# Alpha of the RWKV recurrence loaded by parity into the tile of its product, and r loaded in rows of 1 KB

## Chip, cores and metric

The kernel runs on one core of one Trainium2 chip. The core has TensorE (PE in the profile, with its weight loads as PEld), VectorE (DVE), ScalarE (ACT), GpSimd (POOL) and SyncE (SP), which only issues DMAs here. The metric is the device time of one launch in microseconds, as the median of three runs.

## What is computed

Two layers of an encoder trunk run over 768 tokens (a sequence of 512 and one of 256) with 1024 features. Layer 0 has differential attention (4 heads) and, beside it, a bidirectional RWKV-7 mixer (8 heads of 64), with one output projection for both; layer 1 has dilated attention; each layer ends with a SwiGLU FFN. The change lies in the recurrence of the mixer, which runs forwards and backwards and is summed:

```python
def rwkv_scan(r, w, k, v, kk, a, reverse):
    def step(st, inp):
        r_t, w_t, k_t, v_t, kk_t, a_t = inp
        sa = jnp.einsum('bhvk,bhk->bhv', st, -kk_t)
        st = (st * w_t[:, :, None, :] + sa[..., None] * (kk_t * a_t)[:, :, None, :]
              + v_t[..., None] * k_t[:, :, None, :])
        y = jnp.einsum('bhvk,bhk->bhv', st, r_t)
        return st, y
    _, ys = lax.scan(step, s0, xs, reverse=reverse)
...
y = (rwkv_scan(rh, heads(decay(w0_f, w1_f, w2_f)), heads(k_f), vh, kk, heads(a_f), False)
     + rwkv_scan(rh, heads(decay(w0_b, w1_b, w2_b)), heads(k_b), vh, kk, heads(a_b), True))
```

## The kernel before

The recurrence runs in chunks of 64 tokens: 12 chunks in each direction, 24 units. An earlier stage has worked out, for each chunk, four operands with the decay folded in, and parked them in DRAM: alpha (`AL`, kk with the decay), r (`RH`), the two keys (`KB`, which holds kk·a and k side by side), and `Ti`, the inverse of a triangular matrix. Eight heads lie as four pairs `j` on the free axis; the parity `par` of a head says whether it lies on partitions 0 to 63 or 64 to 127 (`rows`).

A unit has three parts. `fetch` (L938 to L953) issues its DMAs on SP's queue: KB, two halves of RH, AL, two halves of v into the tile `SUV`; `fetch_inverse` (L955) adds Ti. RH goes into one of four standing tiles `rdiag` (L934), 128 x 4 x 128, that hold r on the diagonal blocks and zeros beside them, zeroed once by POOL, so that one matmul over 128 rows serves both heads of a pair. `prep` (L958 to L985) makes what does not depend on the state: the product of KB and RH on PE (bank `pp`, later `gm`), masked by DVE into `LR` (L969); a copy of alpha into `LK` by ACT, one for each parity (L973), and the product of KB and AL, masked by DVE into the other half of LK (L980); KB turned by PE and copied by ACT into `KBT` (L985). `chain` (L987 to L1028) is the serial part: the state S is copied into SUV (L996, one half by ACT and one by DVE), LK and SUV are multiplied into X, ACT copies X to `Xs` (L1001), Ti and Xs give U, copied into SUV (L1008, ACT and DVE), KBT and SUV give the new state (L1014 and the decay in L1015, both DVE), and RH with S plus LR with SUV give y, which goes into `ys` (L1024 by DVE, L1026 by ACT). When both directions have passed a block of 128 tokens, `finish` (L1029 on) normalizes it: a dozen instructions, most on DVE (L1037 to L1050), two on POOL.

`rounds` (L1064) walks the 24 units, forwards and backwards in turn, fetches three units ahead and prepares two ahead. The order on each engine is made by a scheduler that simulates the program with its own estimates when it is built: `chain` has a high priority, `prep` a low one, and the f32r matmuls of projections the lowest, as filling. The first five rounds share the time with the differential attention of the last heads; the other seven run while the weights of the output projection are loaded (`wo`, through `raw` at L134, two buffers) and split into a high and a low part (`split`: ACT's cast at L139, then a subtraction at L140, which for these eight weights is on POOL).

Of the kernel before, what the change touches and what calls it, by code (L numbers as in the profile page):

```python
# [8 lines left out]
F32 = mybir.dt.float32  # L9
F32R = mybir.dt.float32r  # L10
BF16 = mybir.dt.bfloat16
I32 = mybir.dt.int32
# [6 lines left out]
P = 128  # L19
# [35 lines left out]
class Core:  # L55
# [860 lines left out]
    def rwkv(self, rw, park, out):  # L916

        nc, A = self.nc, self.A
        am = []
        for d in "fb":  # L920
            t = rw.tile([P, P], I32, tag="am" + d, name="am" + d)
# [5 lines left out]
        tile = lambda tag, shape, bufs=1: rw.tile(shape, F32, tag=tag, name=self.uid(tag), bufs=bufs)  # L927
# [5 lines left out]

        rdiag = [rw.tile([P, 4, P], F32, tag=f"RH{i}", name=f"RH{i}") for i in range(NB)]  # L934
        for x in rdiag:
            nc.gpsimd.memset(x, 0.0)

        def fetch(di, c):  # L938
            u = {}
            u["AL"] = tile("AL", [P, 4, 64], NB)  # L940
            u["KB"] = tile("KB", [P, 4, 2, 64], NB - 1)
            u["SUV"] = tile("SUV", [P, 4, 2, 64], NB)
            n = units[0]
            units[0] += 1
            u["RH"], u["Ti"] = rdiag[n % NB], tile("Ti", [P, 4, 64], NB)
            nc.sync.dma_start(u["KB"], park["KB"][di, c])
            for rr in rows:
                nc.sync.dma_start(u["RH"][rr, :, rr], park["RH"][di, c, rr])
            nc.sync.dma_start(u["AL"], park["AL"][di, c])
            v = park["v"][64 * c:64 * c + 64].rearrange("t (j h v) -> t j h v", j=4, h=2)  # L950
            nc.sync.dma_start(u["SUV"][64:P, :, 0], v[:, :, 0])
            nc.sync.dma_start(u["SUV"][0:64, :, 1], v[:, :, 1])
            ready[di, c] = u  # L953
# [4 lines left out]
        def prep(di, c):  # L958

            u = ready[di, c]  # L960
            LK, LR, KBT = (tile(n, [P, 4, 2, 64], NB - 1) for n in ("LK", "LR", "KBT"))
            u["LK"], u["LR"], u["KBT"] = LK, LR, KBT
            KB, RH, AL = (u[n] for n in ("KB", "RH", "AL"))
            st = lambda x, j: x[:, j].rearrange("p s t -> p (s t)")
            b = self.bank("pp")
            for j in range(4):
                self.mm(b[:, j * P:(j + 1) * P], st(KB, j), RH[:, j])
            v = b.bitcast(I32).rearrange("p (j x) -> p j x", x=64)
            nc.vector.tensor_tensor(out=LR.rearrange("p j h x -> p (j h) x").bitcast(I32), in0=v,  # L969
                                    in1=am[di][:, 64:P].unsqueeze(1).to_broadcast([P, 8, 64]), op=ALU.bitwise_and)  # L970
            for par in range(2):
                rr = rows[par]
                nc.scalar.copy(out=LK[rr, :, par], in_=AL[rr])  # L973
            b = self.bank("pp")
            for j, par in heads:
                self.mm(b[rows[1 - par], j * 64:(j + 1) * 64], KB[rows[par], j, 1 - par], AL[rows[par], j])
            v = b[:, 0:256].bitcast(I32).rearrange("p (j x) -> p j x", x=64)
            for par in range(2):
                rr = rows[par]
                nc.vector.tensor_tensor(out=LK[rr, :, 1 - par].bitcast(I32), in0=v[rr],  # L980
                                        in1=am[di][rr, 0:64].unsqueeze(1).to_broadcast([64, 4, 64]), op=ALU.bitwise_and)
# [5 lines left out]
        def chain(di, c, first, last):  # L987
# [10 lines left out]
            for j, par in heads:  # L998
                self.mm(xb[rows[par], j * 64:j * 64 + 64], LK[:, j, par], SUV[:, j, par])
            X = tile("Xs", [P, 256], 2)  # L1000
# [18 lines left out]
            for j, par in heads:  # L1019
                y = yb[o, j * P + par * 64:j * P + par * 64 + 64]  # L1020
                self.mm(y, RH[:, j, rows[par]], S[:, j], True, False)
                self.mm(y, LR[:, j, par], SUV[:, j, par], False, True)
# [611 lines left out]
```

## Time and profile before

| what | value |
|---|---|
| runs | 2123.34, 2125.56, 2126.11 us, median 2125.56 |
| the profiled execution | 2126.21 us, its span 2124.4 us |
| PE busy | 2048.7 us, 96% of the span |
| DVE busy | 1378.2 us, 65% |
| ACT busy | 905.9 us, 43% |
| POOL busy | 886.5 us, 42% |
| mean granted TensorE clock | 0.973 of full speed |
| DMA packets | 150227, of them 95926 under 512 B |

The profile is of one execution. A time such as 621.67 counts from the start of its span. Busy time is an average over stages that are bound by different engines, so it says little by itself: what matters is who ends PE's waits in the stretch where the change lies. In a row of waits the engine on the left of the arrow waited, and what stands on the right came last. A row with several shapes gives a mean over them.

### The profile page before, as it was taken

How to read it: one execution, taken by the hardware profiler on the slowest of the kernel's cores; microseconds unless marked ns; L12 is line 12 of the kernel's file. 1: busy time of each engine (PE TensorE's matmuls, PEld its weight loads, DVE VectorE, ACT ScalarE, POOL GpSimd, SP SyncE). 2: the span in 40 equal slices, each digit the busy share in tenths (PEclk: the TensorE clock that was granted, in tenths of full speed). 3: DMA queues.
4: the chain of work that ended last, by engine and by line, in shares of the span. 5: the costliest groups of instructions: out<-in, count | busy, mean ns of one | idle time of the engine just before them, and what ended most of it. 6: DMA issues, size and time to landing. Idle time of an engine off the chain costs nothing. (4 is left out here: it accounts for less than half of the span.)

```text
span 2124.4 us, 33739 instructions
## 1 busy us (share of the span) xinstructions
PE 2048.7 (96%) x13270; PEld 1772.5 (83%) x13270; DVE 1378.2 (65%) x2147; ACT 905.9 (43%) x1703; POOL 886.5 (42%) x833
## 2 busy tenths in 40 slices
PE   7999999999998989999999999999998999999998
PEld 7767776777887778999999998888677999999997
DVE  5456996856579566566666657543568566666665
ACT  5467555447554254433333335222444433333332
POOL 4344341653113156543444535443137544543442
PEclk9999997999999999999999999999999999999999
DMA  4334434114365311211222235221131222221124
GB/s 156 87 75 90 97 74 137 55 26 144 84 184 161 129 64 61 80 60 60 73 77 70 72 137 193 74 71 38 51 109 60 71 79 70 70 69 60 60 80 149
DMA packets 150227, 189.01 MB, mean 89 GB/s; under 512 B 95926, under 2 KB 107784, under 8 KB 150068
## 3 DMA queue, kind: packets, MB, share of 16 engines
q1 hardware_dynamic: 126880, 168.00, 25.4%
q10 hardware_dynamic: 20372, 12.03, 2.0%
q0 software_dynamic: 2816, 6.83, 1.0%
q8 instruction: 104, 1.70, 0.3%
q14 instruction: 55, 0.45, 0.1%
HBM read 150.20 MB, written 36.23 MB: 88 GB/s over the span
## 5 line engine op out<-in xcount | busy, mean ns | idle before, releaser
L83 PE MATMUL gm<-xh,w 128*128 128x384 f32 x896 | 249.1, 342 | 2.8 <-ACT xh L139 2.8
L140 DVE TENSOR_TENSOR wl<-wraw,wh 128x1024 fp32r<-128x1024 f32 (+1 forms) x96 | 126.0, 1313 | 151.7 <-ACT wh L139 150.3
L83 PE MATMUL gm<-T,w 128*128 128x384 f32 x1032 | 203.6, 340 | 7.9 <-ACT w L139 7.3
L83 PE MATMUL gm<-xh,wh 128*128 128x256 f32 (+3 forms) x640 | 208.8, 348 | 0.8 <-ACT pad L489 0.8
L83 PE MATMUL gm<-xl,wh 128*128 128x256 f32 (+3 forms) x640 | 207.6, 348 | 0.0
L83 PE MATMUL gm<-xh,wl 128*128 128x256 f32 (+3 forms) x640 | 206.1, 346 | 0.0
L140 DVE TENSOR_TENSOR w<-S,w 128x512 fp32r<-128x512 f32 x176 | 168.8, 961 | 43.8 <-ACT w L139 36.4
L83 PEld LDWEIGHTS gm<-T,w 128*128 128x128 f32 x1032 | 184.1, 188 | 12.7 <-ACT w L139 8.5
L139 ACT CAST wh<-wraw 128x1024 fp32r<-128x1024 f32 (+1 forms) x103 | 107.5, 1046 | 163.8 <-PE gm L83 96.8
L139 ACT CAST w<-S 128x512 fp32r<-128x512 f32 x176 | 108.9, 621 | 156.7 <-POOL S L291 54.6
L83 PEld LDWEIGHTS gm<-xh,w 128*128 128x128 f32 x896 | 167.3, 192 | 7.7 <-ACT xh L139 3.6
L139 ACT CAST w<-wraw 128x512 fp32r<-128x512 f32 x126 | 76.0, 620 | 206.7 <-PE gm L83 138.1
L83 PE MATMUL gm<-xl,w 128*128 128x384 f32 x448 | 153.4, 342 | 3.0 <-DVE xl L140 3.0
L293 POOL TENSOR_TENSOR S<-wraw,S 128x512 f32<-128x512 f32 x42 | 62.8, 1496 | 204.8 <-DVE w L140 204.8
L140 DVE TENSOR_TENSOR w<-wraw,w 128x512 fp32r<-128x512 f32 x126 | 117.5, 949 | 38.1 <-ACT w L139 37.9
L83 PE MATMUL sc<-xh,w 128*128 128x384 f32 x512 | 140.8, 336 | 1.0 <-DVE u L330 1.0
L83 PEld LDWEIGHTS gm<-xh,wh 128*128 128x128 f32 (+1 forms) x640 | 120.2, 194 | 21.8 <-issue 5.8
L83 PEld LDWEIGHTS gm<-xh,wl 128*128 128x128 f32 (+1 forms) x640 | 119.9, 194 | 20.6 <-issue 7.0
L83 PEld LDWEIGHTS gm<-xl,wh 128*128 128x128 f32 (+1 forms) x640 | 120.0, 194 | 19.7 <-issue 7.3
L392 DVE TENSOR_TENSOR acc<-acc,ob 128x512 f32<-128x512 f32 x128 | 87.4, 683 | 66.6 <-PE ob L83 65.5
L83 PE MATMUL sc<-T,w 128*128 128x384 f32 x552 | 111.2, 340 | 7.4 <-ACT v L350 3.3
L348 POOL TENSOR_TENSOR sil<-sil,v 128x384 f32<-128x384 f32 x44 | 46.9, 1066 | 163.1 <-DVE v L330 162.9
(502 smaller groups left out, 5301.5 us busy)
## 6 DMA issues: line engine op xcount, KB each, us to landing
wraw<-in_gate SPq DMA_DIRECT2D x44, 512.0 KB, 3.4
wraw<-in_down SPq DMA_DIRECT2D x44, 512.0 KB, 3.7
wraw<-in_up SPq DMA_DIRECT2D x40, 512.0 KB, 3.5
wraw<-in_wqk SPq DMA_DIRECT2D x20, 512.0 KB, 3.7
wraw<-in_wo SPq DMA_DIRECT2D x14, 512.0 KB, 4.0
wraw<-in_wrkv SPq DMA_DIRECT2D x12, 512.0 KB, 3.5
KB<-pkKB SPq DMA_DIRECT2D x24, 256.0 KB, 3.2
pkx<-x SPq DMA_DIRECT2D x12, 512.0 KB, 3.4
```

The source lines that it names most:

```text
L83: return self.nc.tensor.matmul(o, a, b, start=start, stop=stop)
L139: self.nc.scalar.copy(out=hi, in_=x)
L140: (eng or self.nc.vector).tensor_tensor(out=lo, in0=x, in1=hi.bitcast(F32), op=ALU.subtract)
L293: eng.tensor_tensor(out=s2, in0=a12, in1=s2, op=ALU.subtract)
L348: nc.gpsimd.tensor_tensor(out=o, in0=o, in1=a[0], op=ALU.mult)
L392: nc.vector.tensor_tensor(out=accs[t][:, fs], in0=accs[t][:, fs], in1=os[t, f], op=ALU.add)
```

## The change

Alpha is no longer loaded into a tile of its own and copied. `LK` becomes a tile that is fetched: its layout is now parity, pair, time instead of pair, parity, time; two DMAs put alpha of each parity onto its 64 partitions, and the product still fills the other half. LK has four buffers instead of three, and the four of AL are gone. `rdiag` has the same layout, parity, pair, time, so that the half of a parity is one run of 4 x 64 numbers on each partition, 1 KB, instead of four runs of 256 B. The matmuls read the same numbers from their new places; that of KB and RH takes its moving operand in two runs of 64.

```diff
-        rdiag = [rw.tile([P, 4, P], F32, tag=f"RH{i}", name=f"RH{i}") for i in range(NB)]
+        rdiag = [rw.tile([P, 2, 4, 64], F32, tag=f"RH{i}", name=f"RH{i}") for i in range(NB)]
...
-            u["AL"] = tile("AL", [P, 4, 64], NB)
+            u["LK"] = tile("LK", [P, 2, 4, 64], NB)
...
-            for rr in rows:
-                nc.sync.dma_start(u["RH"][rr, :, rr], park["RH"][di, c, rr])
-            nc.sync.dma_start(u["AL"], park["AL"][di, c])
+            for par, rr in enumerate(rows):
+                nc.sync.dma_start(u["RH"][rr, par], park["RH"][di, c, rr])
+                nc.sync.dma_start(u["LK"][rr, par], park["AL"][di, c, rr])
...
-                self.mm(b[:, j * P:(j + 1) * P], st(KB, j), RH[:, j])
+                self.mm(b[:, j * P:(j + 1) * P].rearrange("p (h t) -> p h t", h=2), st(KB, j), RH[:, :, j])
...
-            for par in range(2):
-                rr = rows[par]
-                nc.scalar.copy(out=LK[rr, :, par], in_=AL[rr])
...
-                self.mm(b[rows[1 - par], j * 64:(j + 1) * 64], KB[rows[par], j, 1 - par], AL[rows[par], j])
+                self.mm(b[rows[1 - par], j * 64:(j + 1) * 64], KB[rows[par], j, 1 - par], LK[rows[par], par, j])
...
-                nc.vector.tensor_tensor(out=LK[rr, :, 1 - par].bitcast(I32), in0=v[rr],
+                nc.vector.tensor_tensor(out=LK[rr, 1 - par].bitcast(I32), in0=v[rr],
...
-                self.mm(xb[rows[par], j * 64:j * 64 + 64], LK[:, j, par], SUV[:, j, par])
+                self.mm(xb[rows[par], j * 64:j * 64 + 64], LK[:, par, j], SUV[:, j, par])
...
-                self.mm(y, RH[:, j, rows[par]], S[:, j], True, False)
+                self.mm(y, RH[:, par, j], S[:, j], True, False)
```

The scheduler then makes a new order. Outside the recurrence it differs only in a few places at the start of the first FFN and around the second output projection. On ACT, in the rounds beside the loads of the output projection's weights (`wh` is the high part of such a weight, `gq` a square in `finish`), there stood before:

```order
L1001 COPY Xs_6287<-sc_6278 128x256
L973 COPY LK_6423<-AL_6265 64x4x64 x2
L996 COPY SUV_6027<-S_967_6189 64x4x64
L1008 COPY SUV_5921<-sc_6289 64x4x64
L985 COPY KBT_6332<-gm_6352 128x512
L1001 COPY Xs_6380<-ob_6371 128x256
L973 COPY LK_6504<-AL_6358 64x4x64 x2
L1040 ACTIVATE gq_6120<-ys_4980 128x512
L139 CAST wh_6878<-wraw_6876 128x1024
L985 COPY KBT_6425<-gm_6445 128x512
```

And now, on ACT at the same chunks (the lines are three lower):

```order
L139 CAST wh_6845<-wraw_6843 128x1024
L993 COPY SUV_6004<-S_954_6165 64x4x64
L1037 ACTIVATE gq_6095<-ys_4980 128x512
L998 COPY Xs_6261<-sc_6252 128x256
L139 CAST wh_6851<-wraw_6849 128x1024
L139 CAST wh_6857<-wraw_6855 128x1024
L1005 COPY SUV_5900<-sc_6263 64x4x64
L982 COPY KBT_6187<-gm_6205 128x512
L998 COPY Xs_6352<-ob_6343 128x256
L139 CAST wh_6863<-wraw_6861 128x1024
```

The copies into LK are gone, and four casts of weights stand where there was one. On POOL, in the same rounds (`wl` and `xwl` are the low parts, the steps on `var` and `gst` belong to a `finish`), there stood before:

```order
L140 TENSOR_TENSOR wl_6879<-wraw_6876,wh_6878 128x1024
L156 TENSOR_SCALAR var_6127<-gst_6118 128x8
L994 MEMSET S_1057_6678 128x256
L140 TENSOR_TENSOR wl_6885<-wraw_6882,wh_6884 128x1024
L157 TENSOR_TENSOR gst_6118<-var_6127,mh 128x8
L994 MEMSET S_1074_6773 128x256
L140 TENSOR_TENSOR wl_6891<-wraw_6888,wh_6890 128x1024
L156 TENSOR_SCALAR var_6247<-gst_6238 128x8
L157 TENSOR_TENSOR gst_6238<-var_6247,mh 128x8
L140 TENSOR_TENSOR wl_6897<-wraw_6894,wh_6896 128x1024
```

And now, on POOL:

```order
L140 TENSOR_TENSOR wl_6840<-wraw_6837,wh_6839 128x1024
L140 TENSOR_TENSOR wl_6846<-wraw_6843,wh_6845 128x1024
L156 TENSOR_SCALAR var_6102<-gst_6093 128x8
L157 TENSOR_TENSOR gst_6093<-var_6102,mh 128x8
L140 TENSOR_TENSOR wl_6852<-wraw_6849,wh_6851 128x1024
L140 TENSOR_TENSOR wl_6858<-wraw_6855,wh_6857 128x1024
L140 TENSOR_TENSOR wl_6864<-wraw_6861,wh_6863 128x1024
L991 MEMSET S_1039_6644 128x256
L140 TENSOR_TENSOR xwl_6868<-wraw_6869,xwh_6867 128x1024
L156 TENSOR_SCALAR var_6220<-gst_6211 128x8
```

Six of the eight splits now stand ahead of the second `finish`, where three did, and five ahead of the first clearing of S, where one did. On SP, the loads of the third and fourth of these weights (each waits for a split, since there are two raw buffers), there stood before:

```order
L949 DMA AL_6762<-pkAL 128x256
L946 DMA KB_6668<-pkKB 128x512
L134 DMA wraw_6888<-in_wo 128x1024
L134 DMA wraw_6894<-in_wo 128x1024
```

And now, on SP, from the first weight to the fetch behind the fourth:

```order
L134 DMA wraw_6837<-in_wo 128x1024
L134 DMA wraw_6843<-in_wo 128x1024
L946 DMA KB_6239<-pkKB 128x512
L948 DMA RH_4983<-pkRH 64x256 x2
L951 DMA SUV_6122<-pkv 64x4x64
L952 DMA SUV_6122<-pkv 64x4x64
L134 DMA wraw_6849<-in_wo 128x1024
L134 DMA wraw_6855<-in_wo 128x1024
L1041 DMA gq_6105<-pkg 128x512
L949 DMA LK_6329<-pkAL 64x256
L948 DMA RH_4984<-pkRH 64x256 x2
```

The third and fourth load now stand one fetch of RH behind the first two, where there were two; the fetch of r and alpha that follows stands behind them on the queue.

## Rows read from the trace of the kernel before

**Rows 1.** The page, part 1: busy us, share of the span, instructions.

```profile
PE 2048.7 (96%) x13270; PEld 1772.5 (83%) x13270; DVE 1378.2 (65%) x2147; ACT 905.9 (43%) x1703; POOL 886.5 (42%) x833
```

**Rows 2.** Stretches: length, busy PE, PEld, DVE, ACT, POOL, granted clock, DMA.

```profile
500.00:600.00 100.00, 98.93 (x1312) 81.89 (x1313) 60.74 (x149) 63.12 (x176) 17.92 (x53) 1.00 0.40 112
600.00:620.00 20.00, 18.89 (x344) 16.69 (x342) 16.03 (x32) 11.67 (x26) 0.00 (x0) 1.00 0.71 211
620.00:680.00 60.00, 50.78 (x820) 44.05 (x816) 58.03 (x90) 31.49 (x65) 27.97 (x18) 1.00 0.66 193
680.00:700.00 20.00, 20.00 (x267) 16.22 (x267) 9.43 (x20) 3.38 (x8) 0.00 (x0) 1.00 0.09 33
```

**Rows 3.** Waits of PE, 600 to 680: us in total, times, longest us.

```profile
PE ob L84 <- DVE SUV L1008: 2.8, 3, 2.1
PE gm L84 <- DMA RH<-pkRH: 2.0, 3, 0.8
PE sc L84 <- DVE SUV L1008: 2.0, 1, 2.0
PE sc L84 <- ACT SUV L996: 1.2, 1, 1.2
PE ob L84 <- ACT SUV L996: 0.8, 1, 0.8
```

**Rows 4.** Instructions on LK: the copies, ns min/median/max, first and last start.

```profile
L973 ACT COPY LK<-AL x48: 401/402/427, 490.4 to 675.1; 64x256 f32<-64x256 f32 x48
```

**Rows 5.** Issues of RH and AL in ns; DMAs 470 to 700, us to landing.

```profile
L948 SPq DMA_DIRECT2D RH<-pkRH x48: 512/518/847, 486.2 to 675.2; - x48
L949 SPq DMA_DIRECT2D AL<-pkAL x24: 320/422/1469, 477.5 to 663.4; - x24
AL<-pkAL SPq DMA_DIRECT2D x24, 128.0 KB, 3.1
RH<-pkRH SPq DMA_DIRECT2D x48, 64.0 KB, 2.5
Ti<-pkTi SPq DMA_DIRECT2D x24, 128.0 KB, 2.4
```

**Rows 6.** The page, part 5: groups with count, busy us, mean ns, idle before.

```profile
L83 PE MATMUL gm<-xh,w 128*128 128x384 f32 x896 | 249.1, 342 | 2.8 <-ACT xh L139 2.8
L83 PE MATMUL gm<-T,w 128*128 128x384 f32 x1032 | 203.6, 340 | 7.9 <-ACT w L139 7.3
```

**Rows 7.** Timeline of POOL and of DVE at 621: start us, us, instruction.

```profile
621.18 2.35 POOL L140 TENSOR_TENSOR wl<-wraw,wh 128x1024 fp32r<-128x1024 f32 x1 [24.26 <-ACT wh L139]
621.67 2.15 DVE L1015 TENSOR_TENSOR S<-S,dc 128x256 f32<-128x256 f32 x1
```

**Rows 8.** DVE groups: five of 600 to 680, then two of 500 to 600.

```profile
L1048 DVE TENSOR_TENSOR ys<-ys,lw 128x512 f32<-128x512 f32 x4 | 6.5, 1629 | 0.1
L996 DVE COPY SUV<-S 64x256 f32<-64x256 f32 x10 | 6.4, 643 | 0.3
L1046 DVE TENSOR_TENSOR gz<-gz,lb 128x512 f32<-128x512 f32 x3 | 6.1, 2022 | 0.1
L1015 DVE TENSOR_TENSOR S<-S,dc 128x256 f32<-128x256 f32 x8 | 5.1, 635 | 0.1
L1050 DVE TENSOR_TENSOR gz<-gz,gq 128x512 f32<-128x512 f32 x3 | 2.1, 686 | 0.0
L1015 DVE TENSOR_TENSOR S<-S,dc 128x256 f32<-128x256 f32 x10 | 4.2, 418 | 0.2
L996 DVE COPY SUV<-S 64x256 f32<-64x256 f32 x10 | 2.9, 293 | 0.3
```

**Rows 9.** Stretches of 2 us, columns as in rows 2.

```profile
482.00:484.00 2.00, 1.12 (x5) 0.57 (x5) 1.84 (x6) 0.53 (x2) 0.31 (x3) 1.00 0.01 4
484.00:486.00 2.00, 2.00 (x7) 1.53 (x8) 0.90 (x4) 1.25 (x4) 1.26 (x6) 0.50 0.20 66
492.00:494.00 2.00, 2.00 (x11) 2.00 (x10) 0.37 (x3) 1.27 (x4) 0.07 (x1) 0.50 0.82 274
```

More of the change, by code (lines that the diff above doesn't have):

```diff
@@ L960, in prep @@
             u = ready[di, c]
-            LK, LR, KBT = (tile(n, [P, 4, 2, 64], NB - 1) for n in ("LK", "LR", "KBT"))
-            u["LK"], u["LR"], u["KBT"] = LK, LR, KBT
-            KB, RH, AL = (u[n] for n in ("KB", "RH", "AL"))
+            LR, KBT = (tile(n, [P, 4, 2, 64], NB - 1) for n in ("LR", "KBT"))
+            u["LR"], u["KBT"] = LR, KBT
+            KB, RH, LK = (u[n] for n in ("KB", "RH", "LK"))
             st = lambda x, j: x[:, j].rearrange("p s t -> p (s t)")
```

## The prediction, made before the changed kernel was run

> **What bounds the kernel now.** I read the page first: TensorE (PE) is busy for 2048.7 us, 96% of the span [rows 1], so whatever the change gives has to come out of PE's idle time, and only where the change acts. That is the recurrence, from about 477 us to 701 us. The table by stretches splits it in two [rows 2]. From 500 to 600 us the recurrence shares PE with the attention of the other heads, and PE is busy for 98.93 of 100 us, the Vector engine (DVE) for 60.74, the Scalar engine (ACT) for 63.12. PE is the bound there, and ACT has room. From 600 to 680 us PE is idle for 1.11 and then 9.22 us, 10.3 us together, while DVE is busy for 58.03 of the last 60 us and ACT for 31.49. DVE is the bound of that stretch. After 680 us PE is full again. So about 10 us can be won, and most of it belongs to DVE, from which the change takes no instruction away.
>
> Who ended PE's waits there [rows 3]: DVE's copy of SUV, 2.8 + 2.0 us; the load of r (RH), 2.0 us in three waits, the longest 0.8; ACT's copy of the state into SUV, 1.2 + 0.8 us. The copies that the change removes are in no row that PE waited for.
>
> **The change part by part.** The 48 copies of alpha into LK take 402 ns each on ACT [rows 4], 48 x 0.402 = 19.3 us of ACT's time. They lie beside PE's and DVE's work: ACT is idle for nearly half of 620 to 680. What they can cost is a place in the queue: ACT runs in order, and a pair, 0.8 us, can stand ahead of the SUV copy that PE waits for. That wait is 2.0 us in all [rows 3]. So the gain is between 0 (the chain hangs on DVE, whose step on the state feeds that copy) and 2.0 us; I take half, 1.0 us.
>
> The loads of r. Before, each half has 64 partitions with four runs of 256 B; now one run of 1 KB. An issue of RH takes 0.518 us on SP's queue, one of alpha 0.422 at the median and 0.320 at the least [rows 5]. A fetch thus spends 2 x 0.518 + 0.422 = 1.46 us on r and alpha before, and afterwards four issues of 0.32 to 0.42, 1.28 to 1.69 us: nothing won or lost on the queue. The landing: RH lands after 2.5 us with 64 KB in 256 B runs, the inverse Ti after 2.4 us with 128 KB in 1 KB runs, alpha after 3.1 with the same [rows 5]. So the longer run is worth 0.1 us by Ti, and by alpha nothing. The three RH waits bound the term: 0 if landing stays, 2.0 us if all three go. I take 0.2 us for each wait, 0.6 us, near the Ti row with its half of the bytes.
>
> The Trainium skill has a rule for this: "DMA: Bandwidth & Descriptors", section Specifications, says that pieces of 512 B or more are needed for line rate and that smaller ones are read, modified and written. By it the longer rows would take the whole RH wait away, and the sum would be 1.4 us lower. The row of RH beside that of Ti shows no such gap.
>
> Alpha, in two loads of 64 partitions where one had 128, adds 24 DMAs. It also comes free later: an AL tile was free after the preparation of its chunk, an LK tile only after the first product of that chunk's chain. But RH of the same chunk waits for the last product of the same chain and is used in the matmuls ahead, so alpha is not what is late: 0 us. At worst it costs waits like those on RH, 2.0 us.
>
> The Trainium skill speaks against this half: "SBUF — State Buffer", section "Can I just issue two DMAs to hit both halves?", holds that two loads on half the partitions each do not overlap. By it alpha would be complete one landing of 2.5 us later, and if that ate the RH gain too, the sum would come out 0.6 us higher. No row here has alpha in halves.
>
> PE's own instructions keep count and size. The moving operand of the r product now lies in two runs of 64 elements. The nearest rows are the FFN's products, whose x operand lies in three runs (342 ns) and whose T operand in one (340) [rows 6]: 192 products at 2 ns are 0.4 us at most, and below nothing there is no reason. I take 0.
>
> The new order. The scheduler plans with the shorter ACT queue, and every engine's order changes through the recurrence. The place that matters is the split of the output projection's weights: ACT casts, GpSimd (POOL) subtracts, eight times, in 2.35 us each. Before, three of them come ahead of the second normalization and the others are spread behind it; now six stand ahead of it, nearly together, and their loads with them. What one does to DVE can be seen at 621 us [rows 7]: the split starts at 621.18, DVE's step on the state at 621.67, and that takes 2.15 us. The grouped rows give the total [rows 8]: L1015 635 ns against 418 in the stretch before (8 times), the SUV copy L996 643 against 293 (10 times), L1046 and L1048 2022 and 1629 against 686 of their like L1050 (3 and 4 times): 1.7 + 3.5 + 4.0 + 3.8 = 13.0 us of DVE's time from 600 to 680, 1.6 us a split. The splits stay eight, so the 13.0 us stay too, but some move into 600 to 620, where DVE is busy for 16.03 of 20 us [rows 2]: at most 4 us won. Against it, there they meet the chain's own steps and not the normalization's. I take 1.0 us won, nearest to nothing because DVE's work stays; the bounds are 6 us won (those 4, and 2 of PE's waits on SUV with them) and 6 us lost (the slower rival).
>
> The sum on the profiled execution, 2126.2 us: 1.0 + 0.6 + 0 + 0 + 1.0 = 2.6 us, so 2123.6. The median of the runs, 2125.6, lies 0.6 us below that execution: 2123.0 us.
>
> **The rivals.** First, more is won: PE's idle 10.3 us hang on DVE, and splits that leave the full stretch free its bound. With 6 us for the order, 1.0 + 0.6 + 6 = 7.6 us less than 2125.6, 2118 us. For it: DVE has 4 us idle ahead of the full stretch and 2 us in its 60. Against it: no DVE instruction goes away.
>
> Second, slower. Six splits together on DVE's chain steps: the one shown at 621 stopped such a step, and PE's longest wait on SUV is 2.1 us [rows 3]. Four more of these are 4 x 2.1 = 8.4 us, less the 2.6 us won, 5.8 us more: 2131 us. The loads add to it: raw weights have two buffers, so the third and fourth load wait on SP's queue for the first two splits, and the fetches of r and alpha stand behind them. It decides from the point at which two or more of the group's splits stop steps of the chain while PE has no other work ready. A fall of the clock would go the same way: at 482 PE was busy for 1.12 of 2 us, and then the granted clock is 0.50, that is 1.2 GHz, in five rows of 2 us, the first and last of which are shown [rows 9]; that is 5 us of work at 2.4 GHz. The 2.1 us waits after 600 did not bring it.
>
> Third, nothing: the copies filled ACT's spare time, RH lands as before, the order gives nothing; 2125.5 us.
>
> Fourth, the change does not do what it says: the loads come later, alpha's second half behind r, RH's waits of 2.0 us double and the other gains go under; about 2127 us.
>
> **How the numbers follow.** Forecast (2123.0, own range 2120 to 2126): 0.36, of which 0.08 lies below 2121.3. More won: 0.26. Slower: 0.23. Nothing: 0.10. Loads later: 0.05. A measurement of this kernel can tell about 0.2% from no change, 4.25 us: below 2121.3 is faster, above 2129.8 slower. Faster 0.26 + 0.08 = 0.34; slower 0.23; within 0.28 + 0.10 + 0.05 = 0.43. The range has to take in most of both outer cases: from 2114 us (all 10.3 us of idle time gone, and 1 us of spread) to 2132 us (the slower rival and 1 us of spread).
>
> **What would show it.** In the profile after: ACT's busy time 19 us lower and no row of LK on ACT; issues of RH near 0.4 us; 48 x 256 = 12288 packets under 512 B less. PE's wait on RH near 1.4 us or gone. The splits of GpSimd close together after 600, and with them either long rows of DVE on the state with PE waiting on SUV (slower), or DVE below 58 of 60 us afterwards and PE fuller (more won). If PE's idle time from 600 to 680 stays near 10 us and the time still moves by more than 4 us, what failed lies outside the recurrence, in the small reorderings at the start of the first FFN or around the second output projection, which I took as 0.

## The result, and the profile after

The changed kernel is slower: 2140.03 us, the median of 11 runs (2131.14 to 2147.44), against 2126.11 us for the kernel before in the same sessions (11 runs, 2115.35 to 2131.78). The ratio is 1.0070, with a 95% interval from 1.0051 to 1.0089. The profiled execution took 2137.71 us, its span is 2135.9. The forecast was 2123.0 with a range up to 2132, so the time lies 8 us outside it, on the side of the second rival.

First what the edit itself did. This is part 1 of the page of the changed kernel (busy us, share, instructions) and the page's row on packets:

```profile
PE 2054.6 (96%) x13270; PEld 1779.0 (83%) x13270; DVE 1384.1 (65%) x2147; ACT 888.8 (42%) x1655; POOL 884.1 (41%) x833
DMA packets 141394, 189.00 MB, mean 88 GB/s; under 512 B 84022, under 2 KB 98952, under 8 KB 141236
```

And the row of the groups by line on the issues of RH (ns, least/median/most, then the first and the last start):

```profile
L948 SPq DMA_DIRECT2D RH<-pkRH x48: 444/532/1666, 488.3 to 692.4; - x48
```

ACT is busy for 17.1 us less than in [rows 1] and has 48 instructions less: the copies of [rows 4] are gone. PE has the same 13270 matmuls. The issues of RH did not get shorter: 532 ns against 518 in [rows 5].

Where the time went is in the stretches that answer to [rows 2] (length, busy PE, PEld, DVE, ACT, POOL, granted clock, DMA):

```profile
500.00:600.00 100.00, 99.58 (x1214) 81.12 (x1212) 57.94 (x139) 52.94 (x145) 15.80 (x50) 0.95 0.39 108
600.00:620.00 20.00, 15.11 (x214) 13.05 (x213) 8.60 (x15) 7.41 (x17) 1.08 (x3) 0.91 0.50 150
620.00:680.00 60.00, 50.27 (x763) 44.30 (x764) 56.11 (x92) 24.29 (x46) 25.44 (x16) 0.91 0.62 184
680.00:700.00 20.00, 17.19 (x323) 15.11 (x324) 15.95 (x33) 6.35 (x15) 1.83 (x2) 1.00 0.58 165
```

Read the clock column first. In [rows 2] it is 1.00 in all four; here it is 0.95, 0.91, 0.91. From 500 to 600 us PE is even busier than before, and yet it got through 1214 matmul records where it had got through 1312: a full PE at a lower clock does less (the clock is 5% lower there, the records are 7% fewer). From 600 to 680 PE is idle for 14.6 us where it was idle for 10.3. The waits of that stretch, which answer to [rows 3] (us in total, times, longest), have other heads:

```profile
PE gm L84 <- DVE LR L969: 3.1, 2, 2.8
PE tr L87 <- DVE o L901: 2.7, 1, 2.7
PE ob L84 <- ACT SUV L1005: 1.9, 1, 1.9
PE sc L84 <- DMA RH<-pkRH: 1.9, 1, 1.9
PE sc L84 <- ACT Xs L998: 1.4, 1, 1.4
```

Line numbers from prep on are 3 lower than before. The mask step on LR and the attention's own step on o (its tail now lies behind 600 us) have taken the place of DVE's SUV copy. The row of `sc` on the load of RH has to be read with care: the matmul that waited there multiplies SUV and KBT and does not read RH. The timelines of PE and ACT show what came last:

```profile
632.49 0.33 PE L84 MATMUL sc<-SUV,KBT 128*64 128x64 f32 x2 [1.87 <-DMA RH<-pkRH]
631.12 1.04 ACT L139 CAST wh<-wraw 128x1024 fp32r<-128x1024 f32 x1 [1.17 <-DMA wraw<-in_wo]
632.08 0.36 ACT L1005 COPY SUV<-sc 64x256 f32<-64x256 f32 x1
```

The chain's copy into SUV stood on ACT behind the cast of a wo weight, which had waited 1.17 us for its load.

To follow the loss through the program I took the starts of four PE instructions from the timeline: the first r product of prep, the attention's last transposes of o, the recurrence's last y product, and the first product of the first FFN. Between them lie 104.8, 101.8 and 88.9 us before, and 116.2, 106.7 and 90.6 after: 11.4 us are lost beside the attention, 4.9 behind it, 1.7 on the way to the FFN. The parts ahead and behind came out 6.5 us shorter in this execution. So in these two executions most of the loss lies in the 100 us in which PE was full.

### The profile page after: what moved, and what is told of

It is laid out like the page before. It is cut to its first block, busy times and chain, and to the rows that moved or that the text cites. A ratio compares the mean times of both kernels' runs of the same rounds, so it can differ in the third digit from the quotient of the medians.

```text
span 2135.9 us, 33745 instructions
## 1 busy us (share of the span) xinstructions
PE 2054.6 (96%) x13270; PEld 1779.0 (83%) x13270; DVE 1384.1 (65%) x2147; ACT 888.8 (42%) x1655; POOL 884.1 (41%) x833
## 5 line engine op out<-in xcount | busy, mean ns | idle before, releaser
L140 DVE TENSOR_TENSOR w<-wraw,w 128x512 fp32r<-128x512 f32 x126 | 118.2, 955 | 40.4 <-ACT w L139 40.1
L83 PE MATMUL sc<-T,w 128*128 128x384 f32 x552 | 111.2, 340 | 5.2 <-ACT v L350 3.3
```

The source lines that it names most:

```text
L83: return self.nc.tensor.matmul(o, a, b, start=start, stop=stop)
L140: (eng or self.nc.vector).tensor_tensor(out=lo, in0=x, in1=hi.bitcast(F32), op=ALU.subtract)
```

## Experiments

**Loads or order.** The edit changes two things: what is transferred, and the order that the planner makes. They can be parted. The framework takes edges between two instructions of one engine that order their issue and wait for nothing; a table of the order of one kernel, put as a chain of such edges on the other, holds each engine to it:

```
+    traced = [i for i in tc.nc.cur_bb.bb.instructions if type(i).__name__.startswith("Inst")]
+    for e in ("PE", "DVE", "Activation", "Pool", "SP"):
...
+        mine = [i for i in traced if str(i.engine).split(".")[1] == e]
+        for x, y in zip(at, at[1:]):
+            tc.add_manual_dep(mine[y], mine[x].name, edge(), reason="order")
```

All kernels below are made that way, but for the two with one part alone and the two with one idle line; those have the order that the planner makes of them.

> The changed kernel, with every engine's instructions held in the order of the kernel before by edges of order alone (the two LK loads of a unit stand behind its two RH loads, the 48 copies are gone). Theory 'order': the loss is made by the planner's new order, so this kernel stands at the kernel before, ratio 0.998 to 1.002, no fall of the granted clock and under 6 us of idle PE more than before between 600 and 640 us. Theory 'loads': the new transfers (48 LK loads for 24 AL, other rows of RH) delay the recurrence wherever they stand, so the loss stays, ratio 1.005 to 1.009. Theory 'both': between the two, 1.002 to 1.005.

2126.55 us (12 runs), ratio 1.0007, from 0.9991 to 1.0023. The loss is gone. Its stretches:

```profile
500.00:600.00 100.00, 98.93 (x1314) 81.86 (x1314) 60.87 (x149) 55.04 (x154) 18.11 (x53) 1.00 0.39 111
600.00:620.00 20.00, 18.97 (x343) 16.80 (x339) 16.34 (x33) 8.52 (x18) 0.00 (x0) 1.00 0.58 181
620.00:680.00 60.00, 51.53 (x841) 44.62 (x837) 56.62 (x90) 25.76 (x51) 28.59 (x18) 1.00 0.69 211
```

But for ACT's column these are [rows 2] again. PE idles for 9.5 us from 600 to 680 instead of 10.3.

> The kernel before, with every engine's instructions held in the order of the changed kernel (the AL load of a unit stands where its second LK load stood, the two ACT copies of a unit ahead of the first ACT step that could need them). Theory 'order': the loss comes with the order alone, ratio 1.004 to 1.010, with idle PE near 605 and 620 to 636 us and the clock at 1.2 GHz for some microseconds between 560 and 640 us. Theory 'loads': no loss, 0.998 to 1.002.

2156.26 us (4 runs), ratio 1.0147, from 1.0122 to 1.0171. The old transfers in the new order lose, and more than the changed kernel does. Here the 48 copies stand in an order that was made without them, which may be why; no run tests that. Together the two runs settle the first question: the order makes the loss, and the transfers make none that can be told from nothing (from 1.9 us won to 4.9 lost).

**Each part alone,** with the order that the planner makes of it.

```
-            u["AL"] = tile("AL", [P, 4, 64], NB)
+            u["LK"] = tile("LK", [P, 2, 4, 64], NB)
...
-        rdiag = [rw.tile([P, 4, P], F32, tag=f"RH{i}", name=f"RH{i}") for i in range(NB)]
+        rdiag = [rw.tile([P, 2, 4, 64], F32, tag=f"RH{i}", name=f"RH{i}") for i in range(NB)]
```

> Only the alpha part: LK by parity and loaded directly, RH as before; the planner makes an order of its own. Theory 'order': the two parts have no sizes of their own that can be seen, the time goes by what this order happens to be, somewhere from 0.997 to 1.009. Theory 'loads' with the alpha loads as its cause: 1.005 to 1.009.

> Only the RH part: longer rows, AL and the 48 ACT copies as before; the planner makes an order of its own. Theory 'order': somewhere from 0.997 to 1.009, by its order. Theory 'loads' with alpha as the cause: 0.997 to 1.001; with the RH rows as the cause: 1.005 to 1.009.

2142.40 us (1.0082, from 1.0055 to 1.0109) and 2141.77 us (1.0080, from 1.0059 to 1.0102). Each part costs as much as both together, which two causes that add could not do. The orders do not resemble each other: beside the attention the first takes 105.9 us and the second 110.4, where the changed kernel took 116.2. The packets show what the halves cost: alpha alone adds 384 packets under 512 B (96310 against 95926), r alone takes away the 12288 that the prediction named.

**Ahead of the attention's end, or behind it.** Two kernels with one order up to its last store and the other from there.

> New loads; every engine in the changed kernel's order up to the attention's last store of pko (609 us in its trace), from there in the order of the kernel before. Working in the two profiled runs: PE idle plus half of the time at 1.2 GHz is 1.0 us more in 480 to 600 us (13.7 against 10.2 us at 1.2 GHz, idle 2.3 against 3.1) and 13.9 us more in 600 to 720 (idle 17.4 against 10.3, 13.6 against 0.0 us at 1.2 GHz), some of it at 605 to 612 where the attention ends. Theory 'split': the rounds beside the attention lose up to 612 us about 6 us, the rest behind it: 2132, 2129 to 2135. Theory 'wo': all is lost behind the attention, beside the wo splits: 2126, 2123 to 2129. Theory 'attention': all is lost ahead: 2140, 2136 to 2144.

2141.65 us, ratio 1.0067 (1.0053 to 1.0082), beside the attention 116.2 us as in the changed kernel. The new order of that part alone costs about what the whole change costs.

> New loads; the order of the kernel before up to the attention's last store, the changed kernel's from there. Theory 'split': 2134, 2130 to 2137. Theory 'wo': 2140, 2136 to 2144. Theory 'attention': 2126, 2123 to 2129.

2138.29 us, ratio 1.0048 (1.0029 to 1.0067). It costs too, but this cut cannot be taken at its word, as a later one shows:

> New loads; the old order up to the recurrence's 15th copy into Xs on ACT (626.9 us in the kernel with all of the old order), the new order from there. Comparing the starts of these copies, the kernel with the new order from the attention's end on is 0.0 us behind at the 11th, 2.4 at the 12th, 10.1 at the 13th, 16.5 at the 14th, 15.1 at the 15th and 12.0 at the last. Theory 'first third': the loss behind the attention arises between 600 and 642 us, and what follows gives a little back, so with the cut at the 15th the time is that of the old order or less: 2125, 2122 to 2128. Theory 'throughout': the new order is worse in all of the recurrence's second part: 2131 to 2138.

2135.86 us, ratio 1.0036 (1.0023 to 1.0049), and in its trace the recurrence's 16th copy into Xs starts 22.9 us behind the 15th, where the old order has 4.5 and the new one 8.8. At the seam stands everything that the one order had put off and the other had done already. So such cuts price the seam as well, and of the three only the first, whose loss lies ahead of its seam, is clean.

**What happens beside the attention.** In the changed kernel the granted clock falls in the midst of it. Stretches of 4 us:

```profile
556.00:560.00 4.00, 4.00 (x63) 3.20 (x63) 2.12 (x7) 2.66 (x8) 0.52 (x3) 1.00 0.67 194
560.00:564.00 4.00, 4.00 (x36) 3.22 (x34) 2.00 (x5) 1.56 (x6) 0.33 (x2) 1.00 0.29 75
564.00:568.00 4.00, 4.00 (x22) 2.83 (x22) 0.46 (x2) 1.21 (x6) 1.27 (x4) 0.58 0.00 0
568.00:572.00 4.00, 4.00 (x37) 3.43 (x38) 3.77 (x11) 1.12 (x3) 0.00 (x0) 0.50 0.36 98
572.00:576.00 4.00, 4.00 (x41) 3.48 (x41) 0.60 (x3) 1.55 (x3) 0.00 (x0) 0.64 0.18 49
```

PE's column shows no gap. What does stand there is this, in PE's timeline (start us, us, instruction, count of records; a matmul here has two):

```profile
560.88 0.61 PE L84 MATMUL pp<-RH,KB 128*128 128x128 f32 x4
...
562.48 0.33 PE L84 MATMUL cb<-SUV,KBT 128*64 128x64 f32 x2
562.73 0.32 PE L84 MATMUL cf<-Xs,Ti 64*64 64x64 f32 x2
562.99 0.33 PE L84 MATMUL cb<-SUV,KBT 128*64 128x64 f32 x2
563.25 0.33 PE L84 MATMUL cf<-Xs,Ti 64*64 64x64 f32 x2
...
564.53 1.15 PE L84 MATMUL ob<-va,pT 128*128 128x128 f32 x4
```

The state matmuls of one direction (128 rows) and the Ti matmuls of the other (64 rows) stand in turn, and each start is 0.255 us behind the last. Then four records of the shape that took 0.61 us for four at 560.88 take 1.15: the clock is at 1.2 GHz. Every kernel here with the new order of this part and no repair has that place and that fall at its end, five of five; the kernel before has neither the place nor the fall beside the attention. One experiment takes the place away, one puts it into the old order:

```
-2834 cb<-SUV,KBT x1; cf<-Xs,Ti x3; cb<-SUV,KBT x1; cf<-Xs,Ti x1; ...
+2834 cb<-SUV,KBT x8; cf<-Xs,Ti x8; ...
```

> The changed kernel in its own order with one stretch of 20 PE instructions rearranged. At 561.9 us of its trace the 8 state matmuls of one direction (cb from SUV, KBT) and 8 Ti matmuls of the other (cf from Xs, Ti) stand in turn, 24 records in 2.7 us where such records in a row take 0.05 us each, and from 564 us the clock is at 1.2 GHz for 10.3 us with PE busy throughout. Here the 8 state matmuls come first, then the 8 Ti matmuls. Theory 'alternation': that fall goes (half of 10.3 us) and 1.4 us of matmul time with it: 2133, 2130 to 2137, and the stretch from the first prep matmul to the attention's last transposes is 109 to 111 us instead of 116.2. Theory 'elsewhere': the fall comes for another reason and stays, or comes a little later: 2138 to 2142.

2134.26 us (12 runs), ratio 1.0034 (1.0017 to 1.0051). The fall is gone and the part beside the attention takes 109.9 us, within the 109 to 111 expected. The 32 records now take 1.3 us. PE's timeline:

```profile
557.96 0.69 PE L84 MATMUL cb<-SUV,KBT 128*64 128x64 f32 x16
558.58 0.68 PE L84 MATMUL cf<-Xs,Ti 64*64 64x64 f32 x16
```

And two of its stretches of 4 us:

```profile
560.00:564.00 4.00, 4.00 (x56) 3.40 (x55) 3.46 (x10) 2.43 (x9) 1.37 (x5) 1.00 0.39 98
564.00:568.00 4.00, 4.00 (x54) 3.25 (x53) 2.57 (x7) 2.21 (x6) 0.00 (x0) 1.00 0.29 69
```

The profiled execution did not keep all of it: behind the attention it took 111.2 us where the changed kernel took 106.7, with 20.5 us at 1.2 GHz against 13.4, and the wait of the state matmuls on ACT's copy into SUV grew from 1.9 to 4.6 us. The 0.36% between the two ratios is what is left over many runs.

> New loads in the order of the kernel before (2126.6 us), with 16 PE instructions at 528.8 us rearranged: the 8 state matmuls (cf from SUV, KBT) and the 8 Ti matmuls (cb from Xs, Ti) that stand there group behind group now stand in turn. Theory 'alternation': a fall to 1.2 GHz of 8 to 11 us begins at its end, near 532 us, and the time rises by half of that and by 1.3 us: 2132, 2129 to 2135. Theory 'elsewhere': no fall, only the 1.3 us: 2126 to 2129.

2130.05 us (12 runs), ratio 1.0021 (1.0006 to 1.0035). The time lies in the range of the first theory, but there is no fall, as the second has it; and the interval overlaps that of the same order without the alternation (0.9991 to 1.0023). The alternation itself is longer than forecast: its 32 records run from 526.10 to 530.22 us, 4.1 us for what took 1.4 in a row, and the part beside the attention takes 108.0 us instead of 104.8. Its stretches:

```profile
526.00:530.00 4.00, 4.00 (x35) 2.89 (x33) 0.46 (x1) 1.15 (x3) 0.00 (x0) 1.00 0.53 178
530.00:534.00 4.00, 4.00 (x58) 3.45 (x59) 3.73 (x10) 2.50 (x6) 0.62 (x3) 1.00 0.33 98
```

So the alternation costs its own time in both places, and in the changed kernel the fall needs it (or the order of the 20 instructions that were moved with it); but it does not bring a fall by itself. Two other traces make a closer pair that says the same. Behind the attention the kernel before alternates as well, LK's product of one direction (128 rows) with the Ti product of the other (64 rows), each start again some 0.255 us behind the last, from 639.97 to 643.31 us. The kernel before with one idle line, which comes below, has the same row of matmuls from 644.32 to 647.66. The stretches of the one and then of the other:

```profile
640.00:644.00 4.00, 4.00 (x35) 3.13 (x35) 3.90 (x6) 1.77 (x4) 3.83 (x4) 1.00 0.94 241
644.00:648.00 4.00, 4.00 (x59) 3.32 (x59) 3.89 (x6) 1.98 (x5) 1.15 (x1) 1.00 0.69 206
644.00:648.00 4.00, 4.00 (x40) 3.05 (x39) 3.90 (x6) 1.84 (x4) 3.83 (x4) 1.00 0.90 260
648.00:652.00 4.00, 4.00 (x42) 3.26 (x40) 3.91 (x5) 1.19 (x4) 1.58 (x1) 0.57 0.85 226
```

The same matmuls end once at full clock and once in a fall, with PE busy for 4.00 of 4.00 us in all four. What else belongs to a fall is open.

The Trainium skill says in "TensorE: Matmul & The Clock Gate", section "The mechanism" of the part on packing, that a weight load overlaps with a matmul in flight only where it goes to other rows of the array; the same section also names a second buffer for weights as a way past one. The first alone would let 64-row matmuls on other rows overlap and hold up a 128-row one behind any other. The rows agree with half of that: in turn the shapes cost 0.13 us a record, and the 64-row ones in a row 0.04; but the 128-row ones in a row cost 0.04 too, so what the change of shape costs is not explained by it.

**What the falls cost.** If a fall matters, filling PE's idle time should keep the clock up.

```
+def keep_warm(C, bank, x, n):
+    ps, tag, k = C.banks[bank]
+    b = ps.tile([P, 512], F32, tag=tag, name=C.uid("warm"), bufs=k)
+    for i in range(n):
+        C.mm(b, C.ident, x)
```

> The changed kernel in its own order with 28 matmuls of ident and a constant, read by nobody, put where PE stood idle: 6 ahead of the attention's last transposes (idle 2.75 us), 22 ahead of the six waits of 0.9 to 2.8 us between 617 and 636 us. Theory 'clock': the falls to 1.2 GHz at 608, 622 and 632 us cost half of their 13.6 us, and they come because PE ran dry: they vanish, and the time falls by 4 to 7 us to 2133 to 2136. Theory 'waits': what delays the recurrence is the waits themselves and the low clock is hidden in them: 2138 to 2143. If a filler stands in the way of the chain, up to 3 us more in both.

2148.63 us, ratio 1.0098 (1.0081 to 1.0116): slower than without. I had mis-sized the filler: each matmul has two records, 56 in all, and in the profile the 12 beside the attention start 0.43 us apart, so the 28 took 24 us instead of 12. The groups by line, those of the filler behind the attention:

```profile
L84 PE MATMUL warm<-lw,ident x44: 592/592/697, 615.5 to 640.9; 128*128 128x512 f32 x44
```

And the stretch from 600 to 720:

```profile
600.00:720.00 120.00, 114.54 (x1511) 88.48 (x1509) 84.95 (x144) 39.75 (x82) 28.84 (x21) 0.99 0.47 139
```

It still says something. The three falls from 608 to 640 us went (clock 0.99 where the changed kernel has 0.94), idle time from 600 to 720 went from 17.4 to 5.5 us, and the time at 1.2 GHz there from 13.6 to 3.4. Paid 24 us, got back 12 of idle time and half of 10.2: 7 us worse by that sum, 8.6 measured. A fill of the right size was not tried.

That sum can be held against other kernels. From stretches of 2 us between 480 and 860 us, PE's idle time and the time at 1.2 GHz, half of which is counted as lost (an upper price: the 16 records on LK and KB took 0.68 us at full clock, at 556.87 us of the changed kernel, and 1.12 at 567.85):

| kernel | idle | at 1.2 GHz | idle + half | span |
|---|---|---|---|---|
| before | 29.2 | 20.5 | 39.5 | 2124.4 |
| new_loads_old_order | 28.1 | 23.9 | 40.1 | 2124.5 |
| after | 32.5 | 37.5 | 51.3 | 2135.9 |
| new_order_untwined | 33.7 | 34.1 | 50.8 | 2134.1 |
| old_loads_new_order | 42.9 | 61.4 | 73.6 | 2158.4 |

From before to after it grows by 11.8 us and the span by 11.5; with the old loads in the new order by 34.1 and 34.0. The other fifteen kernels do not all agree so well: seven come within 2.5 us of their span, and eight miss by 3 to 11 us (the changed kernel with an idle line, of which more below, has 1.0 us for 9.3, the cut at the 15th copy 14.9 for 4.0, the filled one 19.7 with its 24 of filler for 25.1). So the sum is no rule, and an agreement to 0.3 us is in part luck. For the changed kernel it holds between the four starts of above too, 17.3 of 18.0 us. By it about 70% of the changed kernel's loss is clock (8.5 of 11.8 us, and 11.9 of the 17.3). That does not make the clock a cause apart from the waits: the falls behind the attention went when its idle time was filled.

**Behind the attention.** Here the prediction's second rival had its place: six subtractions of wo weights on POOL close together, beside DVE's steps. They do stand so in the changed kernel, and DVE's steps beside them are long. POOL's timeline:

```profile
622.54 5.00 POOL L140 TENSOR_TENSOR wl<-wraw,wh 128x1024 fp32r<-128x1024 f32 x2 [14.63 <-ACT wh L139]
631.44 5.11 POOL L140 TENSOR_TENSOR wl<-wraw,wh 128x1024 fp32r<-128x1024 f32 x2
```

And DVE's:

```profile
631.51 2.82 DVE L1044 TENSOR_TENSOR ys<-ys,gst 128x512 f32<-128x512 f32 x1 [1.46 <-POOL gst L157]
...
637.21 0.43 DVE L1005 COPY SUV<-sc 64x256 f32<-64x256 f32 x1
...
639.17 0.68 DVE L1036 TENSOR_TENSOR ys<-ys,gst 128x512 f32<-128x512 f32 x1
```

Two steps of one shape on ys take 2.82 us beside POOL and 0.68 alone, and the chain's other copy into SUV, whose matmuls were done at 629.9, stands behind them until 637.21. I moved the copies ahead first, then the subtractions. The copies, in the new order on DVE and ACT, each as soon as its operand can be there; a piece of ACT's:

```
+L993 COPY SUV_5900<-S_933_6047 64x4x64
 L982 COPY KBT_6069<-gm_6087 128x512
 L139 CAST wh_6839<-wraw_6837 128x1024
-L993 COPY SUV_5900<-S_933_6047 64x4x64
+L993 COPY SUV_6004<-S_954_6165 64x4x64
 L139 CAST wh_6845<-wraw_6843 128x1024
-L993 COPY SUV_6004<-S_954_6165 64x4x64
```

> The changed kernel in its own order, but behind the attention each of the chain's steps on DVE and ACT (the copies into SUV and Xs, the two steps of S) stands directly behind the instruction that gives it its data, ahead of the wo casts, pko splits, masks and finish steps that the new order had put ahead of it; PE, POOL and SP keep the new order. Theory 'queue': the idle of PE from 617 to 636 us is chain copies that stand behind such work (the copy at 637.2 us was ready at 629.9); idle in 600 to 720 us falls from 17 to about 10 us and two of the three clock falls go: 2130, 2126 to 2134. Theory 'loads late': PE waits for RH and wo loads and for masks, so nothing is won: 2138 to 2143.

2143.76 us, ratio 1.0077 (1.0062 to 1.0093): nothing won. The waits of PE from 600 to 660 show other ones in their place:

```profile
PE sc L84 <- ACT SUV L1005: 3.0, 1, 3.0
PE tr L87 <- DVE o L901: 2.8, 1, 2.8
PE sc L84 <- DVE LK L977: 2.3, 1, 2.3
PE gm L84 <- ACT KBT L982: 2.2, 1, 2.2
```

Beside the attention's step on o, the heads of the list are now ACT's copy of SUV, the mask on LK and KBT; the chain's copies had been put ahead of such masks and KBT copies. Then the casts, subtractions and loads of the weights, in the order of the second cut, put back to where the old order has them; a piece of POOL's:

```
+L991 MEMSET S_1039_6644 128x256
 L140 TENSOR_TENSOR wl_6840<-wraw_6837,wh_6839 128x1024
 L140 TENSOR_TENSOR wl_6846<-wraw_6843,wh_6845 128x1024
...
-L140 TENSOR_TENSOR wl_6852<-wraw_6849,wh_6851 128x1024
-L140 TENSOR_TENSOR wl_6858<-wraw_6855,wh_6857 128x1024
```

> The order that is old up to the attention's last store and new from there (2138.3 us), with the eight wo loads (SP), casts (ACT) and subtractions (POOL) moved to where the order of the kernel before has them, by the last chain copy on ACT ahead of each; all else as it was. Theory 'wo': the loss behind the attention is the casts that stand ahead of chain copies on ACT and the subtractions on POOL beside the finish steps on DVE (2.8 us where they take 0.7 alone): 2128, 2125 to 2131. Theory 'finish': it is the place of the pko splits, finish and prep steps, and the wo steps only fill gaps: 2135 to 2141.

2140.25 us, ratio 1.0070 (1.0049 to 1.0090), no better than the 2138.29 without the move. The subtractions did come apart in POOL's timeline:

```profile
630.12 2.35 POOL L140 TENSOR_TENSOR wl<-wraw,wh 128x1024 fp32r<-128x1024 f32 x1
634.47 2.36 POOL L140 TENSOR_TENSOR wl<-wraw,wh 128x1024 fp32r<-128x1024 f32 x1 [2.00 <-ACT wh L139]
648.83 2.36 POOL L140 TENSOR_TENSOR wl<-wraw,wh 128x1024 fp32r<-128x1024 f32 x1 [8.61 <-DMA SUV<-pkv]
```

The same move in the untwined kernel:

> The changed kernel in its own order with both repairs, the untwined stretch and the wo steps at the places of the order before. Theory 'alternation and wo': the gains add, about 6 and 4 us: 2130, 2127 to 2134. If one of the two is not a cause: 2133 to 2137. If neither is: 2138 to 2143.

2135.75 us, ratio 1.0047 (1.0028 to 1.0067): the gain of the untwined stretch alone, and none beside it. The mechanism of my second rival is there, but taking it away wins nothing: in this last kernel PE's longest waits from 600 to 720 us are two on RH, 4.0 us together, and one of 3.5 on a step of DVE on ys.

Then the chain's steps ahead of everything, on PE too, where its two directions take turns: in the second cut, in that with the weights moved and SP's whole queue there put back to the old order, and in the old order. A piece of PE's of the last:

```
-L84 MATMUL sc_6016<-SUV_5718,LK_5716 64x64 x8
-L84 MATMUL ob_6134<-SUV_5809,LK_5807 64x64 x8
+L84 MATMUL sc_6016<-SUV_5718,LK_5716 64x64
+L84 MATMUL ob_6134<-SUV_5809,LK_5807 64x64
+L84 MATMUL sc_6016<-SUV_5718,LK_5716 64x64
```

> The order that is old up to the attention's last store and new from there (2138.3 us), with all steps of the chain on PE, DVE and ACT placed directly behind what gives them their data, and prep, finish, pko and wo work behind them. Theory 'queue': chain steps stand behind other work on the three engines, on PE behind prep matmuls that wait for a mask: 2129, 2126 to 2133. Theory 'amount': the work beside the chain has to be done anyway, and the chain only waits for it elsewhere: 2136 to 2142.

> As the run before, and the pko and wo loads, casts and subtractions and the recurrence's own loads at the places of the old order too: of the new order only the places of prep, masks and finish are left behind the attention. Theory 'queue': 2128, 2125 to 2132. Theory 'transfers' (what the chain waits for are loads that the new order issues behind others): this one gains against the run before, 2126 to 2130 against 2136 to 2142. Theory 'amount': both 2136 to 2142.

> New loads in the order of the kernel before (2126.6 us), with the chain's steps on PE, DVE and ACT behind the attention placed directly behind what gives them their data: a try at a kernel that beats both. If chain steps behind other work cost time in the old order too: 2117 to 2123. If the old order has them where they should be, 2124 to 2129. If prep and finish come too late by it: 2130 to 2136.

2178.08, 2190.03 and 2182.41 us, ratios 1.0224 (1.0205 to 1.0243), 1.0286 (1.0270 to 1.0301) and 1.0251 (1.0237 to 1.0265). All three theories fall. With the chain always first, PE waits for the chain and at times for prep; from 600 to 720 us of the last:

```profile
600.00:720.00 120.00, 84.56 (x1172) 74.04 (x1174) 67.43 (x116) 34.34 (x66) 26.16 (x16) 0.80 0.42 127
```

PE idles for 35.4 us and the clock is 0.80. Of PE's waits there 20.9 us are for the chain's own copies and steps of S, and 6.7 for prep's masks on LK and LR. (The turns themselves are not the cause: all of 128 rows, 30 records on LK start within 0.9 us at 601, 0.03 us a record.) So an order is not good here because the chain comes first. I read it so that prep has to be done while the chain waits; no run tests that alone. Which instructions of the new order spoil that behind the attention stays open.

**Is the new order bad, or the old one good?** One line that computes nothing that is used, 24 copies of 0.19 us on ACT, and changes the plan:

```
+            nc.scalar.copy(out=tile("nil", [P, 1], 2), in_=KB[:, 0, 0, 0:1])
```

> The kernel before with one line more: in prep, ACT copies one element a partition (128x1) of KB into a tile that nobody reads, 24 copies, some 0.2 us each, on an engine that was busy for 906 of 2124 us. The planner, which counts them, makes another order of it: 774 PE, 121 DVE and 100 ACT instructions stand elsewhere. Theory 'picked order': the order of the kernel before is better than most that the planner comes to, and any edit costs what the edit of this case cost: 2132 to 2143. Theory 'this order': the planner's orders are mostly alike and the changed kernel's one is bad: 2125 to 2130.

> The same line in the changed kernel: 1050 PE, 352 DVE and 139 ACT instructions stand elsewhere than in the changed kernel. Theory 'picked order': 2132 to 2145, by its order. Theory 'this order': 2125 to 2131, since it leaves the bad order.

2133.64 us, ratio 1.0018 (1.0003 to 1.0033), and 2132.33 us, ratio 1.0024 (1.0010 to 1.0037), 12 runs each. By the ranges stated both times lie in that of the first theory, near its lower end, but the kernel before read 2128.61 us beside them, so both theories hold by half. An idle line in the kernel before costs about a quarter of what the edit cost, and the same line in the changed kernel wins back two thirds of the loss. Of the six orders that the planner made of kernels here, the old one is the best; the others cost 0.18, 0.24, 0.70, 0.80 and 0.82%. No kernel here beats the kernel before.

## Why the prediction was wrong

**Where it failed: the term for the new order,** which I put at 1.0 us won, between 6 won and 6 lost. The same loads in the two orders took 2126.55 and 2140.03 us: 13.5 us lost. Two steps in it were wrong.

The first was to look for the order's effect only between 600 and 680 us. From 500 to 600 PE was busy for 98.93 of 100 us [rows 2], and I took a full PE as a stretch with nothing to win or lose. The page says busy, not fast. 11.4 us were lost there. The untwined kernel shows 6.3 of them at one place of 16 matmuls, though its trace loses 4.5 again behind the attention; where the other 5.1 went is open.

The second was to price the clock at nothing. I had the row of a fall in hand, 5 us of work lost at 484 to 494 [rows 9], and set it aside because waits of 2.1 us behind 600 had brought none. In the other order more of them came: 37.5 us at 1.2 GHz between 480 and 860 against 20.5.

**The second rival had the right side and the wrong cause.** Its 2131 us came from the grouped subtractions; they were found grouped, DVE's steps beside them were long as [rows 7, 8] had shown, and moving them apart won nothing (2140.25 against 2138.29, 2135.75 against 2134.26). That it came within 9 us of the measured time is luck. The rival's other half, the loads, is there as well: the cast that held up the chain's copy at 632.08 us was waiting for a wo load. Putting the copies ahead of the casts won nothing either (2143.76).

**The other terms.** Copies 1.0, RH 0.6 and alpha 0 made 1.6 us won; with the order held, the measured ratio makes 1.5 us lost, with an interval from 1.9 won to 4.9 lost, so 1.6 won is barely inside and not seen. Single rows say more. The copies: PE's wait on ACT's copy of the state was 2.0 us in [rows 3] and is 1.4 + 0.8 in the held order, so the half of it that I gave the copies does not show. PE's wait on RH went up, not away (2.0 in [rows 3]):

```profile
PE gm L84 <- DMA RH<-pkRH: 3.0, 3, 1.7
PE sc L84 <- ACT SUV L993: 1.4, 1, 1.4
PE ob L84 <- ACT SUV L993: 0.8, 1, 0.8
```

RH with its 1 KB rows lands after 2.3 us at the median where it took 2.5 [rows 5]. Alpha in halves lands after 2.2 us in the held order and 2.7 in the changed kernel, where the whole took 3.1 (2.8 in the kernel with r alone). The Trainium skill's rule that halves do not overlap, which I had weighed in the prediction from "SBUF — State Buffer", section "Can I just issue two DMAs to hit both halves?", would have had it later. PE's waits for LK in that stretch are 0.5 us in all. The issues on SP's queue were mis-sized: 0.47 us for RH and 0.59 for alpha in the held order, so four of them take 2.1 us a fetch, and not the 1.28 to 1.69 of the prediction. The fourth rival is out: with the order held the loads did not cost a time that can be seen. The rival "nothing", 2125.5 us, is what the two edits are worth in the order that was there, as far as these runs can tell.

Of the signs that I had named, ACT's busy time (17 us less), the packets and the grouped subtractions came; RH's issues near 0.4 us did not. The last sign, that a move of over 4 us with unchanged idle time would point to the FFN, did not arise, since the idle time rose by 4.3 us; nor would it have pointed there, for from the first FFN on all kernels here took 1330 to 1340 us, the kernel before 1334 and the changed one 1330.

## What to carry to other kernels

Where a planner orders the instructions, an edit is two edits: what it says, and the new order. Hold the order and time the edit alone, and time a line that does nothing beside it, before a gain or a loss is put down to what the edit says. A stretch in which an engine is full can still lose time, so read the granted clock beside the busy column. And work that keeps an engine waiting is not always worth moving: here each repair behind the attention gave way to another wait. A sum that fits five traces should be tried on the rest.

## What the runs showed of the hardware

Matmuls of 128 rows and of 64 rows in turn start 0.13 us a record apart, 0.04 in a row: 32 records took 4.1 us instead of 1.3 to 1.4. PE's clock went to 1.2 GHz for 10.3 us behind such a stretch, with PE busy in the records throughout; the same alternation at another place brought none, and a like one, of LK's and Ti's products, ended at 1.00 in the kernel before and at 0.57 in the kernel with one idle line. And 24 copies of one column, 0.19 us each on ACT, changed the planner's order and with it the time, by 3.8 us up in the kernel before (0.18% of 2126) and by 9.8 down in the changed one (0.46%); their own time on ACT, 4.6 us, cannot be what made the second.
